# Another machine model behind the scheduler that orders a four-layer decoder trunk

## The chip, the cores and the metric

The kernel runs on one core of a Trainium2 chip. TensorE does the matmuls (its records are called PE, its weight loads PEld), VectorE (DVE) and ScalarE (ACT) do elementwise work and move results out of PSUM, GpSimd (POOL) does a few small steps, and SyncE (SP) issues the DMAs. Each engine works through its own list of instructions in the order in which they were placed there, and waits at semaphores for what the others make. The metric is device microseconds of one execution, from the median of several runs; lower is better.

## The reference

The input is one sequence of 256 positions of width 1024, in float32. Four layers follow each other. Each has a token mixer and then a SwiGLU feed-forward part (FFN); behind each of the two stands a layer norm of `ALPHA * x + h`. The mixers of layers 0 to 3 are HGRN2, mLSTM, S5 and HGRN2 again.

```python
for i in range(DEPTH):
    kind = i % N_MIXERS
    if kind == 0:
        h = _hgrn2_mixer(x, ...)
    elif kind == 1:
        h = _mlstm_mixer(x, ...)
    else:
        h = _s5_mixer(x, ...)
    x = _layernorm(ALPHA * x + h, ln_g[i, 0], ln_b[i, 0])
    x = _layernorm(ALPHA * x + _swiglu(x, ffn_w_gate_up[i], ffn_w_down[i]), ln_g[i, 1], ln_b[i, 1])
return x

def _swiglu(x, w_gate_up, w_down):
    gate, up = jnp.split(x @ w_gate_up, 2, axis=-1)
    return (jax.nn.silu(gate) * up) @ w_down
```

The HGRN2 mixer is a gated linear recurrence with 8 heads of 128: queries, gates, values and output gates are projections of x, scores between positions are weighted by products of gates, and the normalised heads are projected out. The mLSTM mixer is a matrix memory with exponential gates and a short causal convolution; S5 is a complex diagonal state space in 64 groups. The FFN has 2816 hidden units and is the largest part of the arithmetic.

## The kernel before

**Precision and loads.** Every large product is made of three: both operands are split into a high part that TensorE takes as it is and a low rest, and `mm3` (L152 to L157) adds high by high, low by high and high by low. The weights come from DRAM one megabyte at a time: `stage_next` (L97) issues the DMA on SP's queue (L106) into one of three staging buffers, and `halve` (L126) splits it, the high part on ScalarE (L127), the rest on VectorE (L128). `wstage` keeps this one entry ahead of its use (`AHEAD = 1`), in the order of a plan of all weights (`plan`, L1219). The split parts go to a pool of eight buffers each.

```python
def halve(self, x, hi, lo):
    self.nc.scalar.copy(hi, x)
    self.nc.vector.tensor_tensor(lo, x, hi.bitcast(F32), ALU.subtract)
```

**Stages.** The 256 positions are two halves of 128 rows. `as_part` (L159) multiplies x, transposed, with 512 columns of weights for one or both halves; `ws_block` and `ws_wide` (L172, L180) hold the weights in the array instead and stream both halves of x; `ws_wide` does so for the middle blocks of the FFN (L185 with 512 columns, L188 with 256). PSUM has three kinds of banks: two called "g" (projections), two called "t" (transposes) and four called "a" (scores and sums that last).

The FFN (`ffn`, L266) goes over 11 blocks of 256 hidden units: gate and up products, silu and product, and the down product added into four banks. Its layer norm (`norm`, L214) runs under `high_priority()`; for each half it takes statistics on VectorE, a reciprocal root on GpSimd (L197, L198), scales (L235, L236), transposes on TensorE (L240) and splits the result on ScalarE and VectorE (L259, L260).

HGRN (`hgrn`, L446) projects, then runs the scores of two pairs of heads side by side in seven levels. One level (`hgrn_scores`, L582) is a strided copy on ScalarE (L616), small matmuls (L620, L629), a masked copy on VectorE (L623) and the products of gates (L592). Between the levels the calls hand in pieces of the remaining projections. S5 (`s5`, L1063) goes over eight blocks: input matmuls (L1115), rotations and a scan on VectorE (L1158 to L1169) and output matmuls (L1127). The matrices of S5 are computed ahead, in pieces that run among the FFN blocks of layers 0 and 1 (`s5_prepare`, L842), and pass through DRAM.

**What sets the order.** The kernel names the engine of every instruction, but not its place. While the `with tile.TileContext(...)` block closes, the framework's scheduler places the instructions: it runs the traced program on a model of the chip and gives each engine, out of what is ready on that model, the one with the best priority, which is the order of the calls except inside `high_priority()`. It also places the tiles in the buffers of their pools and draws the waits. Two edges are drawn by hand: each load of an activation table comes behind the users of the table before and ahead of its own users (`table` and `act`, L77 to L95). The program has no control flow; it is one list of instructions.

## Time and profile before

| what | value |
|---|---|
| median of 3 runs | 1273.06 us (1273.02 to 1274.07) |
| the profiled execution's own time | 1272.88 us |
| its span, first to last instruction | 1271.1 us |
| mean granted clock of TensorE | 0.999 |
| instructions | 20366 |
| read from DRAM | 234.99 MB |

The profiled execution is 0.18 us under the median, and 1.8 us of it lie outside the span. In the profile an engine's busy time is the union of its instructions' records. The end of a matmul's record is modelled, and the records of matmuls that follow each other overlap, so a TensorE that is busy throughout need not run at its peak. L12 means line 12 of the kernel. Tiles are named by the program without their buffer numbers: w is a staging buffer, hi and lo its split parts, xx the split and transposed x.

### The profile page before, as it was taken

Reading aid. Unit: us, or ns where it says so; the run is one execution under the profiler, and the core shown is the slowest. Engines: PE = TensorE matmul, PEld = TensorE weight load, DVE = VectorE, ACT = ScalarE, POOL = GpSimd, SP = SyncE. Lnnn points to the kernel's source line nnn. Section 1 sums busy time; section 2 is a strip of 40 time slices with the busy share of each in tenths; the row PEclk is TensorE's granted clock in tenths of the full one; section 3 lists DMA queues with packets and bytes.
Section 4 is the critical chain, followed back from the end, with each engine's and each line's share of the span. In section 5 each row is a group of like instructions: output and inputs, shape, how many; then the busy total and the mean of one; then the engine's idle time right before and its main releaser. Section 6 shows DMA issues by size and latency. Waiting matters only on the chain.

```text
span 1271.1 us, 20366 instructions
## 1 busy us (share of the span) xinstructions
PE 1252.0 (98%) x7939; PEld 1047.4 (82%) x7939; DVE 958.8 (75%) x1716; ACT 711.9 (56%) x1158; POOL 54.6 (4%) x78
## 2 busy tenths in 40 slices
PE   9999999999999999999999999999999999999997
PEld 7977788888798888888878778888879778888885
DVE  6877889876787799866599797666595887766664
ACT  6755576675467555666443355555459654555550
POOL 0000200000200110000000000000010001000001
PEclk9999999999999999999999999999999999999999
DMA  8733465765373276756477647555554432755530
GB/s 312 293 134 134 159 223 207 274 243 199 113 277 134 100 259 224 246 207 244 163 273 277 244 166 247 184 199 183 182 189 185 165 121 106 271 173 192 193 139 33
DMA packets 46463, 249.93 MB, mean 197 GB/s; under 512 B 5632, under 2 KB 10128, under 8 KB 20000
## 3 DMA queue, kind: packets, MB, share of 16 engines
q1 hardware_dynamic: 46240, 248.55, 54.4%
q8 instruction: 62, 1.02, 0.3%
q14 instruction: 33, 0.27, 0.1%
q0 software_dynamic: 128, 0.09, 0.0%
HBM read 234.99 MB, written 13.63 MB: 196 GB/s over the span
## 4 chain that ended last, share of the span: by engine, by line
PE 92%; DVE 3%; ACT 2%; issue 1%; POOL 1%; DMA 0%; POOLq 0%; DVEq 0%; ACTq 0%
PE g L185 19%; PE g L155 10%; PE g L157 10%; PE g L156 10%; PE g L188 10%; PE a L155 9%; PE a L156 9%; PE a L157 8%; PE t L240 1%; PE t L1127 1%; PE g L1115 1%; DVE lo L128 1%; PE a L620 1%; PE t L1024 1%; PE a L505 0%
## 5 line engine op out<-in xcount | busy, mean ns | idle before, releaser
L128 DVE TENSOR_TENSOR lo<-w,hi 128x1024 fp32r<-128x1024 f32 x389 | 472.7, 1222 | 115.3 <-ACT hi L127 108.3
L127 ACT CAST hi<-w 128x1024 fp32r<-128x1024 f32 x389 | 406.6, 1051 | 189.0 <-PE a L156 109.1
L185 PE MATMUL g<-xx,hi 128*128 128x512 f32 x1024 | 358.3, 395 | 0.0
L188 PE MATMUL g<-xx,lo 128*128 128x256 f32 x1024 | 267.5, 281 | 0.0
L185 PEld LDWEIGHTS g<-xx,hi 128*128 128x128 f32 x1024 | 186.9, 188 | 34.3
L188 PEld LDWEIGHTS g<-xx,lo 128*128 128x128 f32 x1024 | 192.4, 188 | 10.4
L155 PE MATMUL g<-hi,xx 128*128 128x512 f32 x416 | 169.3, 408 | 4.0 <-ACT xx L259 2.9
L156 PE MATMUL g<-hi,xx 128*128 128x512 f32 x416 | 166.6, 401 | 0.0
L157 PE MATMUL g<-lo,xx 128*128 128x512 f32 x416 | 166.4, 403 | 0.0
L156 PE MATMUL a<-hi,hl 128*128 128x512 f32 x344 | 135.8, 395 | 0.0
L155 PE MATMUL a<-hi,hh 128*128 128x512 f32 x344 | 135.5, 396 | 0.0
L157 PE MATMUL a<-lo,hh 128*128 128x512 f32 x344 | 135.4, 394 | 0.0
L319 ACT COPY sum<-g 128x256 f32<-128x256 f32 x128 | 47.6, 372 | 141.3 <-PE g L185 141.0
L320 DVE TENSOR_TENSOR sum<-g,sum 128x256 f32<-128x256 f32 x128 | 54.3, 424 | 67.2 <-ACT sum L319 66.7
L155 PEld LDWEIGHTS g<-hi,xx 128*128 128x128 f32 x416 | 78.8, 190 | 22.9 <-ACT xx L259 4.7
L157 PEld LDWEIGHTS g<-lo,xx 128*128 128x128 f32 x416 | 78.7, 189 | 17.9 <-DVE lo L128 0.7
L156 PEld LDWEIGHTS g<-hi,xx 128*128 128x128 f32 x416 | 78.9, 190 | 16.0 <-issue 0.2
L156 PEld LDWEIGHTS a<-hi,hl 128*128 128x128 f32 x344 | 64.8, 188 | 14.9 <-DVE hl L309 0.3
L157 PEld LDWEIGHTS a<-lo,hh 128*128 128x128 f32 x344 | 64.7, 188 | 14.8
L155 PEld LDWEIGHTS a<-hi,hh 128*128 128x128 f32 x344 | 64.3, 188 | 13.7 <-ACT hh L308 0.6
L156 PE MATMUL g<-xx,lo 128*128 128x256 f32 x200 | 56.6, 283 | 0.0
L157 PE MATMUL g<-xx,hi 128*128 128x256 f32 x200 | 56.5, 283 | 0.0
(303 smaller groups left out, 1779.4 us busy)
## 6 DMA issues: line engine op xcount, KB each, us to landing
w<-in_w_gu SPq DMA_DIRECT2D x88, 1024.0 KB, 4.9
w<-in_w_dn SPq DMA_DIRECT2D x44, 1024.0 KB, 4.9
w<-in_w_hg SPq DMA_DIRECT2D x30, 1024.0 KB, 5.1
w<-in_w_ml SPq DMA_DIRECT2D x12, 1024.0 KB, 4.9
gb<-in_ln SPq DMA_DIRECT2D x8, 1024.0 KB, 4.7
w<-in_w_ho SPq DMA_DIRECT2D x8, 1024.0 KB, 4.9
w<-in_w_so SPq DMA_DIRECT2D x8, 1024.0 KB, 6.2
ct<-s5ct SPq DMA_DIRECT2D x8, 768.0 KB, 7.8
```

The source lines that it names most:

```text
L127: self.nc.scalar.copy(hi, x)
L128: self.nc.vector.tensor_tensor(lo, x, hi.bitcast(F32), ALU.subtract)
L155: mm(ps, lh, rh, start=start, stop=False)
L156: mm(ps, ll, rh, start=False, stop=False)
L157: mm(ps, lh, rl, start=False, stop=stop)
L185: whole = lambda: mm(ps, hi[:, c], self.xx[:, k].rearrange("p i t -> p (i t)"), start=k == 0, stop=k == KD - 1)
L188: mm(ps[:, S:], lo[:, c], self.xh[:, k], start=False, stop=False)
L240: nc.tensor.transpose(pt[:, (k % 4) * P : (k % 4 + 1) * P], z[:, k * P : (k + 1) * P], self.ident)
L319: nc.scalar.copy(t, ps[:, S:])
L320: nc.vector.tensor_tensor(t, ps[:, 0:S], t, ALU.add)
L620: nc.tensor.matmul(pl[rows(c)].rearrange("p (h a t) -> p a h t", h=2, a=2)[:, i], kk[:, i * P + 32 * c : i * P + 32 * c + 32], view(q, i * ...
L1024: nc.tensor.transpose(ps[:, x * P : (x + 1) * P], k["bz"][:, i, 4 * e + x].rearrange("p j g c -> p (j g c)"), self.ident)
```

## The change

One argument is added where the framework's context is made. It tells the scheduler to run the program on the framework's timeline machine instead of its core machine. The calls that make up the program, their engines, their operands, their priorities and the pools stay as they are.

```diff
     out = nc.dram_tensor("out_x", [S, D], F32, kind="ExternalOutput").ap()
-    with tile.TileContext(nc) as tc:
+    with tile.TileContext(nc, schedule_with_timeline_sim=True) as tc:
         trunk(tc, aps, out)
```

## The prediction

> **What bounds the kernel now.** I read the page first, for the shares of the engines and for the chain of work that ended last.
>
> ```profile
> span 1271.1 us, 20366 instructions
> PE 1252.0 (98%) x7939; PEld 1047.4 (82%) x7939; DVE 958.8 (75%) x1716; ACT 711.9 (56%) x1158; POOL 54.6 (4%) x78
> PEclk9999999999999999999999999999999999999999
> PE 92%; DVE 3%; ACT 2%; issue 1%; POOL 1%; DMA 0%; POOLq 0%; DVEq 0%; ACTq 0%
> ```
>
> The reader is to see one bound: TensorE is busy for 1252.0 of 1271.1 us, its granted clock is full in every slice, and 92% of the last chain is matmuls. No order of the same 7939 matmuls makes them fewer, so an order can only move the time in which TensorE does not work. That time is found stage by stage in the view by stretches (length, then busy us of PE, PEld, DVE, ACT and POOL, granted clock, DMA share, GB/s).
>
> ```profile
> 0.00:53.00 53.00, 50.94 (x375) 45.98 (x375) 36.34 (x42) 41.19 (x59) 1.74 (x8) 1.00 0.85 319
> 53.00:120.00 67.00, 65.71 (x869) 52.40 (x858) 56.14 (x148) 37.98 (x77) 2.08 (x2) 1.00 0.41 147
> 335.00:389.00 54.00, 53.24 (x341) 47.34 (x341) 48.92 (x98) 33.92 (x53) 2.98 (x4) 1.00 0.57 209
> 632.00:660.00 28.00, 26.74 (x124) 20.70 (x123) 26.83 (x47) 15.05 (x21) 3.43 (x4) 1.00 0.65 253
> 660.00:748.00 88.00, 85.72 (x573) 69.80 (x572) 75.31 (x125) 33.31 (x42) 1.72 (x2) 1.00 0.60 221
> 748.00:930.00 182.00, 182.00 (x920) 153.26 (x919) 119.10 (x165) 93.39 (x145) 2.64 (x4) 1.00 0.55 196
> 930.00:985.00 55.00, 53.80 (x379) 49.20 (x378) 40.08 (x58) 43.25 (x71) 3.29 (x5) 1.00 0.58 214
> 985.00:1050.00 65.00, 63.67 (x872) 50.05 (x871) 55.44 (x146) 38.78 (x79) 2.08 (x2) 1.00 0.40 146
> 1261.70:1271.10 9.40, 1.43 (x7) 0.81 (x5) 5.78 (x9) 0.00 (x0) 1.68 (x2) 0.84 0.15 56
> sum 1271.10, PE 1252.03 PEld 1047.37 DVE 958.82 ACT 711.86 POOL 54.60; mean PE 78.25 PEld 65.46 DVE 59.93 ACT 44.49 POOL 3.41
> ```
>
> Length less busy gives the idle time. In all it is 1271.10 - 1252.03 = 19.1 us. The first stretch has 2.1 of it (the first load) and the last 8.0 (the closing layer norm, one dependent chain). That leaves 9.0 us inside, of which six stretches hold 1.29 + 0.76 + 1.26 + 2.28 + 1.20 + 1.33 = 8.1: both score stages of HGRN, the three seams from an FFN into the next mixer, and the S5 blocks. The FFN stretch 748 to 930 has none at all: four such stages are most of the kernel, and order has nothing to give there.
>
> [...]
>
> ```profile
> L128 DVE TENSOR_TENSOR lo<-w,hi 128x1024 fp32r<-128x1024 f32 x389 | 472.7, 1222 | 115.3 <-ACT hi L127 108.3
> L127 ACT CAST hi<-w 128x1024 fp32r<-128x1024 f32 x389 | 406.6, 1051 | 189.0 <-PE a L156 109.1
> L185 PE MATMUL g<-xx,hi 128*128 128x512 f32 x1024 | 358.3, 395 | 0.0
> L155 PE MATMUL g<-hi,xx 128*128 128x512 f32 x416 | 169.3, 408 | 4.0 <-ACT xx L259 2.9
> L156 PE MATMUL g<-hi,xx 128*128 128x512 f32 x416 | 166.6, 401 | 0.0
> L157 PE MATMUL g<-lo,xx 128*128 128x512 f32 x416 | 166.4, 403 | 0.0
> L156 PE MATMUL a<-hi,hl 128*128 128x512 f32 x344 | 135.8, 395 | 0.0
> ```
>
> Matmuls of one shape take 395 ns in the FFN (L185, and L156 into "a") and 408, 401 and 403 in the projections (L155 to L157 into "g"). I take the excess as hidden waits: 416 x (13 + 6 + 8) ns = 11.2 us. So order can return at most 9.0 + 11.2 = 20.2 us, 1.6%, and lose without such a limit.
>
> **The change part by part.** It removes and adds no instruction: 7939 matmuls, 389 pairs of L127 and L128 and every DMA stay, so the sum of the work moves by 0. What may move is each engine's order. The kernel's trace of calls gives a priority (earlier calls first, the layer norms before others), and while the program is built, a model of the chip decides what is ready when an engine comes free. A product is passed over only where that model has its operands late. The edit exchanges the model, hence the places where something is passed over. Where that happens now, the waits of TensorE tell (us in total, times, longest), and the timeline shows one of them:
>
> ```profile
> PE g L155 <- ACT xx L259: 2.9, 5, 0.7
> PE a L620 <- DVE near L623: 2.3, 2, 1.2
> PE t L1127 <- DVE s5hs L1168: 1.3, 1, 1.3
> PE g L155 <- ACT hi L127: 0.9, 1, 0.9
> ```
>
> ```profile
> 94.73 0.40 PE L156 MATMUL g<-hi,xx 128*128 128x512 f32 x1
> 96.30 0.33 PE L620 MATMUL a<-q,kk 128*32 128x32 f32 x16 [1.18 <-DVE near L623]
> 96.56 0.50 PE L157 MATMUL g<-lo,xx 128*128 128x512 f32 x1
> ```
>
> At 94.73 the score step L620 was set too early: TensorE stands 1.18 us, and the next product of the same projection (96.56) stands behind it.
>
> The costs, in turn. **(a) TensorE's own order** in the FFNs: 0, since no stretch there has idle time; the cover is the weight pair split one plan entry ahead. **(b) Order on VectorE and ScalarE** at the six exposed places. Both engines carry the dependent chain and also the splits of weights, which nothing interrupts once begun: 1.222 us on VectorE (L128), 1.051 on ScalarE (L127). The chain at one seam shows what that is like (start, us):
>
> ```profile
> 639.79 1.14 DVE lo L128
> 640.92 0.33 DVE xx L260
> 641.59 1.13 DVE lo L128
> 643.39 1.13 DVE lo L128
> ```
>
> Three splits already lie in this chain. A different readiness puts one more before the chain or takes one out. Behind a split that is put in front wait L260 and the transposes' users on VectorE, and for them the first matmuls of the next projection. Bounds for one place: from -1.35 (the 8.1 us over six places, all regained) to +2.27 (a split on each of both engines). No row of before shows the other order, so this is a choice: one more split of 1.222 us on VectorE at three of the six places, nothing net at the other three: +3.7 us. I lean to loss because five of the six places hold no more than 1.33 us of idle time to give back, while a split on each engine costs 2.27. **(c) Hidden waits**: between -11.2 (all gone) and +11.2 (doubled); near nothing, I take a tenth more, +1.1. **(d) The load queue.**
>
> ```profile
> SPq L106 <- DVE lo L128: 554.1, 102, 21.7
> ```
>
> SP issues each load when a staging buffer is free, so its order is that of the splits. A load moved behind a late split lands late by that split, 1.2 us, and is hidden by the other two staging buffers: 0, and up to 1.2 per place without that cover, inside the bound of (b). POOL is busy 54.6 us and stands only in the layer-norm and head-norm chains, which keep their own order: 0. **(e) Head and tail**: 0; both are one chain of dependent steps with nothing to reorder.
>
> Sum: 3.7 + 1.1 = 4.8 us on the profiled execution's own 1272.88 us, 1277.7. The median of the runs is 1273.06, 0.18 above it, so the forecast is **1277.9 us**, with a range of its own from 1275.6 to 1286.8 (six places at 2.27, 13.6 us).
>
> **The rivals.** *Better aimed order, faster.* The mechanism is the row at 94.73: if the new model has L623 (and L1168 in S5) as late as the chip has it, TensorE takes projection products first and L620 and L1127 afterwards. It decides at these three waits, and it pays as long as there is another product with its weights split; here there is one. It returns 2.3 + 1.3 whole and, for the seams, where TensorE has little else, half of 2.9 + 0.9: 5.5 us, 1267.6. With all 7.4 us of these waits and a quarter of the hidden 11.2, it is 10.2 us, 1262.9. For it speaks that the waits are there and that something stands behind them; against it, that the chains behind are VectorE's, which the new order may as well lengthen.
>
> *No change.* The order may come out the same where it matters, or a gain here pay for a loss there: 1273.1. The FFN rows with no idle time speak for it; against it, that nearly all idle time is in places ruled by order.
>
> *Committed too early, much slower.* A model in which an engine's sequencer takes products before the array is free would choose among what is ready then, and a score step that becomes ready a moment later goes behind products already chosen. The projections are used up early and the later score steps stand bare. One level is these four rows in turn:
>
> ```profile
> L592 DVE TENSOR_TENSOR q<-q,f 128x256 f32<-128x256 f32 (+2 forms) x56 | 24.6, 438 | 0.0
> L592 DVE TENSOR_TENSOR k<-k,f 128x256 f32<-128x256 f32 (+1 forms) x48 | 19.0, 399 | 0.2
> L616 ACT COPY kk<-k 128x256 f32<-128x256 f32 x40 | 15.7, 413 | 11.5 <-DVE k L592 7.9 <-PE a L620 3.5
> L623 DVE COPY_PREDICATED near<-msk,a 128x64 f32<-128x64 int32 x40 | 10.2, 256 | 4.4 <-PE a L620 3.7
> ```
>
> That is 0.438 + 0.399 + 0.413 + 0.256 = 1.51 us a level; there are 7 levels in each of two runs in each of two layers, 28 steps, 42 us. Half of them bare gives 21 us, 1294.1. It decides where fewer than 1.51 / 0.23 = 6.5 matmuls are left between two levels (0.23 us is one matmul's step in the rows below). Nothing in the trace of before speaks for or against how the new model chooses.
>
> *The clock falls.* TensorE starts slowly in this trace: the chain has one matmul each at
>
> ```profile
> 8.16 0.43 PE g L155
> 8.84 0.23 PE g L155
> ```
>
> 0.43 us and then 0.23. Were bare steps long enough to bring that back, each return would cost some 8 matmuls x 0.20 = 1.6 us; ten of them on top of the last rival give 1310. The largest wait inside is 1.3 us and no stretch inside has a clock under 1.00, while the last one, nearly idle, has 0.84. [...]
>
> **How the numbers follow.** Forecast 0.36, better aimed 0.31, no change 0.21, committed early 0.10, clock 0.02. Faster is 0.31, same 0.21, slower 0.36 + 0.10 + 0.02 = 0.48; the bound between them, 0.2% or 2.5 us, is about what a measurement of this kernel can tell from no change. The predicted time is the forecast's, 1277.9. The range from 1263 to 1292 holds the forecast, no change and most of the faster case; it leaves out some 0.05 of that, and 0.10 of the two last.
>
> **What would show it.** Right: PE's busy time within 1 us of 1252.0 plus the hidden waits, idle time grown in the six stretches, with L128 ahead of L260 or the score chain, and FFN stretches with none. The faster rival: the rows L620 <- L623 and L1127 <- L1168 are gone or short. No change: the same waits at the same places. Early commitment: long runs of projection matmuls, then score steps with idle time before each. Wrong altogether would be idle time in an FFN, or waits for a DMA, since both were costed at nothing.

## The result, and the profile after

The changed kernel takes **1376.38 us** (median of 4 runs, 1374.92 to 1377.7) where the kernel before takes 1273.04 beside it: a ratio of 1.0809, with a 95% interval from 1.0791 to 1.0828. The forecast was 1277.9 with a range from 1263 to 1292. The sign is right, and the size is missed twentyfold: 103 us are lost where 4.8 were expected.

The page of the changed kernel first: span, busy time, granted clock, and the chain that ended last.

```profile
span 1375.4 us, 20399 instructions
PE 1284.7 (93%) x7939; PEld 1075.1 (78%) x7939; DVE 963.8 (70%) x1716; ACT 705.0 (51%) x1155; POOL 50.1 (4%) x78
PEclk9998899999999999999998999999999989999998
PE 84%; DVE 11%; ACT 2%; issue 2%; POOL 1%; DMA 0%; POOLq 0%; DVEq 0%; ACTq 0%
```

The work is the same: 7939 matmuls, 1716 instructions on VectorE; ScalarE's 1155 instructions instead of 1158 are three loads of an activation table fewer (15 instead of 18), so the prediction's "removes and adds no instruction" was not quite right. TensorE's idle time grows from 19.1 us to 1375.4 - 1284.7 = 90.7, its busy time by 32.7, together the 104.3 us by which the span grew. VectorE holds 11% of the chain instead of 3%, and the granted clock is no longer full in every slice. The view by stretches (columns as in the prediction; stretches with little or no idle time are left out) shows where.

```profile
104.00:132.00 28.00, 19.14 (x329) 15.38 (x331) 20.72 (x65) 8.51 (x24) 2.00 (x2) 0.76 0.13 47
132.00:159.00 27.00, 23.06 (x141) 18.96 (x130) 16.45 (x28) 10.74 (x17) 4.69 (x5) 0.94 0.28 93
159.00:186.00 27.00, 21.83 (x94) 17.11 (x93) 24.81 (x88) 14.45 (x31) 3.54 (x6) 0.87 0.33 118
186.00:358.00 172.00, 172.00 (x944) 144.23 (x943) 130.02 (x229) 105.09 (x174) 1.81 (x1) 1.00 0.65 225
358.00:388.00 30.00, 22.31 (x93) 16.56 (x92) 19.94 (x51) 7.57 (x14) 6.21 (x10) 0.89 0.30 107
487.00:510.00 23.00, 17.64 (x77) 13.62 (x76) 22.02 (x69) 5.58 (x14) 3.62 (x6) 0.85 0.38 137
684.00:713.00 29.00, 22.97 (x96) 17.31 (x95) 22.74 (x43) 8.49 (x14) 2.30 (x4) 0.88 0.91 360
713.00:806.00 93.00, 87.09 (x558) 72.11 (x557) 72.42 (x113) 31.86 (x38) 0.00 (x0) 0.94 0.47 168
806.00:828.00 22.00, 15.42 (x65) 11.77 (x64) 15.63 (x34) 6.80 (x12) 3.36 (x4) 0.84 0.47 185
1000.00:1028.00 28.00, 22.01 (x100) 16.86 (x99) 21.89 (x42) 9.15 (x16) 3.69 (x7) 0.88 0.40 149
1110.00:1169.00 59.00, 44.23 (x498) 35.31 (x498) 41.06 (x102) 22.71 (x51) 5.96 (x6) 0.88 0.23 87
1169.00:1195.00 26.00, 21.05 (x90) 16.51 (x89) 16.33 (x32) 7.32 (x15) 0.74 (x2) 0.87 0.32 122
1357.00:1375.40 18.40, 8.22 (x36) 6.15 (x34) 11.69 (x20) 0.37 (x1) 3.36 (x4) 0.81 0.15 57
```

The row from 186 to 358 is an FFN: still no idle time, as the prediction had it, and so are the other three. Three rows are what stands at the end of the HGRN scores and behind them (104, 132 and 1110): 8.9 + 3.9 + 14.8 = 27.6 us idle, of which 8.8 are the head norms (L413 in the waits below). Seven are the seams, layer norms between a mixer and an FFN or the other way round (159, 358, 487, 684, 806, 1000, 1169): 5.2 + 7.7 + 5.4 + 6.0 + 6.6 + 6.0 + 5.0 = 41.9. The S5 blocks (713) have 5.9 (2.3 before) and the tail 10.2 (8.0 before). Every row here with idle time also has a lower clock. The waits of TensorE (total us, times, longest) name what it waits for:

```profile
PE t L240 <- DVE xx L260: 18.3, 6, 4.6
PE t L240 <- DVE x L236: 16.2, 7, 6.4
PE t L413 <- DVE on L519: 8.8, 4, 3.9
PE a L620 <- DVE q L592: 8.2, 6, 1.8
PE a L620 <- DVE near L623: 4.2, 3, 2.0
```

Most of it is VectorE: the norms' transposes (L240), the head norms (L413) and the score steps (L620). These five rows hold 55.7 of the 90.7 us.

And the 32.7 us of busy time? They are the clock. The trace records the granted clock itself; in the changed kernel it is at 0.50 in fifteen stretches inside the kernel and in the tail, before in the tail alone (its record begins 9.9 us into the changed kernel and 8.5 us into the one before, behind the start with steps of 0.43 us that both have). The longest of these stretches and the sum of all sixteen (TensorE alone: length, busy, granted clock, DMA share, GB/s):

```profile
119.09:129.33 10.24, 8.57 (x83) 0.50 0.01 2
sum 99.20, PE 70.19; mean PE 4.39
```

TensorE is busy for 70.2 us at a granted clock of 0.50, where a step of 512 columns takes 0.43 us instead of the 0.23 at 1.00. At 1.00 the same matmuls would take about 70.2 x (1 - 0.23 / 0.43) = 33 us less, an estimate that is as large as the whole growth. So some 72 of the 104 us are waits, and some 33 are matmuls at 0.50 behind these waits.

Why do the score steps wait? Each of the next rows is a stretch between one score step and the next, with the matmuls that read xx alone (the projections): first the changed kernel, then the one before.

```profile
65.12:70.19 5.07, 5.07 (x21) 3.88 (x21) 0.00 (x0) 0.00 (x0) 1.00 0.31 92
```

```profile
90.91:92.96 2.05, 2.05 (x8) 1.42 (x8) 0.00 (x0) 0.00 (x0) 1.00 0.00 0
```

Counted over the scores of the first layer, the changed kernel has its projections in eight runs between the score matmuls, four of them of exactly 21 products, and none behind the eighth; before, there are over twenty runs of 1 to 12, with 2 to 4 products still between late steps. A step's chain needs far less cover than 21 (6.5 products by the prediction's estimate), so the products are used up early, and the last steps stand bare. TensorE's timeline there (start, duration, idle time before it and what ended it):

```profile
116.83 0.80 PE L620 MATMUL a<-q,kk 128*32 128x32 f32 x32 [0.81 <-DVE near L623]
119.63 0.91 PE L620 MATMUL a<-q,kk 128*32 128x32 f32 x32 [2.00 <-DVE near L623]
```

At a seam it is the norm that stands bare, and behind S5 it also lasts longer. VectorE's timeline there, the changed kernel first, then the kernel before (some rows left out):

```profile
802.40 0.69 DVE L221 SCALAR_TENSOR_TENSOR x<-x,ho 128x512 f32<-128x512 f32 x1
803.01 1.22 DVE L128 TENSOR_TENSOR lo<-w,hi 128x1024 fp32r<-128x1024 f32 x1
...
805.35 1.21 DVE L128 TENSOR_TENSOR lo<-w,hi 128x1024 fp32r<-128x1024 f32 x1
...
807.08 1.21 DVE L128 TENSOR_TENSOR lo<-w,hi 128x1024 fp32r<-128x1024 f32 x1
...
808.32 2.31 DVE L128 TENSOR_TENSOR lo<-w,hi 128x1024 fp32r<-128x1024 f32 x2
811.14 1.67 DVE L235 SCALAR_TENSOR_TENSOR x<-x,mv,gb 128x256 f32<-128x256 f32 x4
813.33 1.67 DVE L236 SCALAR_TENSOR_TENSOR x<-x,rs,gb 128x256 f32<-128x256 f32 x4
```

```profile
737.39 1.42 DVE L221 SCALAR_TENSOR_TENSOR x<-x,ho 128x512 f32<-128x512 f32 x2
...
740.03 1.17 DVE L128 TENSOR_TENSOR lo<-w,hi 128x1024 fp32r<-128x1024 f32 x1
741.12 0.88 DVE L235 SCALAR_TENSOR_TENSOR x<-x,mv,gb 128x256 f32<-128x256 f32 x2
742.04 0.88 DVE L236 SCALAR_TENSOR_TENSOR x<-x,rs,gb 128x256 f32<-128x256 f32 x2
```

Before, one split lies in this norm. Now there are five, four of them more (4 x 1.2 = 4.9 us). And TensorE has no products left beside it: it stands 6.4 us (the longest wait of the row L240 <- x L236). Before, it had them; the stretch of that norm and what follows it:

```profile
736.00:758.00 22.00, 22.00 (x102) 17.54 (x101) 20.95 (x38) 12.73 (x17) 2.63 (x4) 1.00 0.50 185
```

Here both have their part: the chain is longer, and its cover is gone.

The other seams are of two kinds. Take the chain of the first half from its statistics (L222) to its first L260, the step that TensorE's transposes wait for. At the four seams behind a mixer this chain now holds four splits instead of one, and lasts 10.8 to 13.3 us instead of 5.7 to 7.1. At the three seams behind an FFN it holds two splits instead of three and lasts 8.8 to 10.3 us instead of 8.1 to 8.3; there it is mostly the cover that is missing. An example of the first kind is the seam behind the first HGRN layer, where TensorE stands 4.0 us, until 166.53, for L260; VectorE is at splits from 161.06, 162.59 and 164.94. The last of them and the step behind it:

```profile
164.94 1.21 DVE L128 TENSOR_TENSOR lo<-w,hi 128x1024 fp32r<-128x1024 f32 x1
166.06 0.42 DVE L260 TENSOR_TENSOR xx<-t,xx 128x256 fp32r<-128x256 f32 x1
```

### The profile page after: what moved, and what is told of

Read it like the earlier page. It is cut to its first block, busy times and chain, and to the rows that moved or that the text cites. A ratio compares the mean times of both kernels' runs of the same rounds, so it can differ in the third digit from the quotient of the medians.

```text
span 1375.4 us, 20399 instructions
## 1 busy us (share of the span) xinstructions
PE 1284.7 (93%) x7939; PEld 1075.1 (78%) x7939; DVE 963.8 (70%) x1716; ACT 705.0 (51%) x1155; POOL 50.1 (4%) x78
## 4 chain that ended last, share of the span: by engine, by line
PE 84%; DVE 11%; ACT 2%; issue 2%; POOL 1%; DMA 0%; POOLq 0%; DVEq 0%; ACTq 0%
PE g L185 17%; PE g L156 10%; PE g L155 10%; PE g L157 9%; PE g L188 9%; PE a L155 7%; PE a L156 7%; PE a L157 7%; DVE lo L128 3%; DVE x L221 1%; PE t L1127 1%; DVE st L222 1%; PE g L1115 1%; PE t L240 1%; DVE x L236 1%
## 5 line engine op out<-in xcount | busy, mean ns | idle before, releaser
L185 PE MATMUL g<-xx,hi 128*128 128x512 f32 x1024 | 362.4, 395 | 0.0
L188 PE MATMUL g<-xx,lo 128*128 128x256 f32 x1024 | 267.3, 281 | 0.0
L155 PE MATMUL g<-hi,xx 128*128 128x512 f32 x416 | 169.5, 416 | 4.7 <-ACT xx L259 3.3
L156 PE MATMUL g<-hi,xx 128*128 128x512 f32 x416 | 171.1, 413 | 0.0
L155 PE MATMUL a<-hi,hh 128*128 128x512 f32 x344 | 131.6, 397 | 1.4 <-ACT hh L308 1.4
L155 PEld LDWEIGHTS g<-hi,xx 128*128 128x128 f32 x416 | 80.4, 195 | 23.9 <-ACT xx L259 4.5
L157 PEld LDWEIGHTS g<-lo,xx 128*128 128x128 f32 x416 | 81.7, 196 | 18.3 <-issue 0.2
L156 PEld LDWEIGHTS g<-hi,xx 128*128 128x128 f32 x416 | 82.4, 198 | 16.8
L259 ACT CAST xx<-t 128x256 fp32r<-128x256 f32 x56 | 20.5, 372 | 87.1 <-PE t L240 82.7
L240 PE MATMUL t<-ident,x 128*128 128x128 f32 x112 | 24.9, 314 | 34.6 <-DVE xx L260 18.3
```

The costliest lines, as they stand in the source:

```text
L155: mm(ps, lh, rh, start=start, stop=False)
L156: mm(ps, ll, rh, start=False, stop=False)
L157: mm(ps, lh, rl, start=False, stop=stop)
L185: whole = lambda: mm(ps, hi[:, c], self.xx[:, k].rearrange("p i t -> p (i t)"), start=k == 0, stop=k == KD - 1)
L188: mm(ps[:, S:], lo[:, c], self.xh[:, k], start=False, stop=False)
L240: nc.tensor.transpose(pt[:, (k % 4) * P : (k % 4 + 1) * P], z[:, k * P : (k + 1) * P], self.ident)
```

## The experiments

Two theories of the order and one of the loads were to be told apart. *Choosing ahead*: the timeline machine has a queue for each engine, whose size the runs below set; if what has gone into it is not reordered any more, an instruction with a better priority that becomes ready later goes behind it. *Durations*: the machine prices the instructions wrongly, so that it has a chain ready at the wrong time, whatever the queue. *Loads*: SP's order is the harm. All ratios are against runs of the kernel before on the same chip.

**Smaller queues.** The sizes are set ahead of the context; a, v and p are the sizes for ScalarE, VectorE with GpSimd, and TensorE.

```diff
+    from concourse.engine_type import EngineType as E
+    from concourse.hw_specs import TRN2Spec
+
+    TRN2Spec.ENG_ISSUE_QUEUE_DEPTH = {E.SP: 12, E.Activation: a, E.DVE: v, E.PE: p, E.Pool: v}
```

All sizes 1:

> [...] Theory A, choice too early: the instructions are chosen while others still wait in the queue, so what becomes ready a moment later comes behind them. Then this run gives back most of the 103 us: 1270 to 1290 us, with 3 to 12 projection matmuls between two score levels instead of 21 and no layer-norm seam with more than 2 us of idle TensorE. Theory B, prices: the timeline machine has other durations and semaphore delays, and the order follows from these. Then the time stays above 1350 us. Theory C, clock: idle stretches halve TensorE's clock, and the loss feeds itself; it can be at most the some 15 us of matmuls at 0.43 us in the changed kernel, whatever this run shows.

Measured: 1494.22 us, 1.1722 (1.1701 to 1.1743): far worse, not better. Its bound of 15 us for the clock in the changed kernel counts matmuls of 512 columns alone; over all shapes it is some 33 us, as shown above. TensorE alone at 1:

> The timeline machine with a queue of 1 for TensorE alone; VectorE, ScalarE and GpSimd keep 12. Theory A in the form that TensorE's early choice is the cause (21 matmuls ahead of each score level): back to 1270 to 1290 us. Theory A in the form that VectorE's and ScalarE's early choice is the cause in the layer norms (five weight splits inside the chain of one norm): only the idle time at L620 and L629, some 25 to 35 us, comes back, and the L240 waits stay: 1335 to 1350 us. Theory B: above 1350.

Measured: 1497.95 us, 1.1759 (1.1735 to 1.1782). The projection runs were indeed short (2 to 12 products, counted between the score steps in TensorE's order), but other things went wrong. A stretch inside an FFN of this kernel, then one of its waits:

```profile
200.00:380.00 180.00, 161.36 (x845) 134.76 (x844) 122.56 (x219) 95.75 (x157) 1.80 (x1) 0.93 0.53 184
```

```profile
PE g L155 <- DVE hd L296: 21.9, 3, 11.2
```

The FFN itself now stands 18.6 us, and on the product with the gate (L296): something in the order of VectorE or ScalarE, or of TensorE against them, is wrong that was not before. So these two runs don't decide on choosing ahead; they change a second thing.

The elementwise engines alone at 1, TensorE at 35:

> The timeline machine with a queue of 1 for VectorE, ScalarE and GpSimd; TensorE keeps 35. Theory A by TensorE: above 1350 us. Theory A by the elementwise engines: the waits of L240 (34.6 us in the changed kernel) and of L413 (8.8) go and the score levels stay bare, 1300 to 1325 us. Theory B: above 1350.

Measured: 1339.86 us, 1.0518 (1.0497 to 1.0539): some 37 of the 103 us come back, less than theory A by the elementwise engines had. VectorE alone at 1:

> The timeline machine with a queue of 1 for VectorE alone. If the weight splits put into the norm chains on VectorE (L128 between L221, L222 and L235) are the larger part, this is within 10 us of the run with all three elementwise engines at 1; if ScalarE's early choice matters as much, it lies halfway between that run and the changed kernel's 1376.

Measured: 1344.59 us, 1.0555 (1.0534 to 1.0576), so most of that, 32 us, is VectorE. In the kernel with all three at 1 the waits say what it is:

```profile
PE t L240 <- DVE x L236: 6.5, 8, 3.7
PE t L240 <- DVE xx L260: 3.4, 3, 1.3
```

The norms' waits fall from 16.2 + 18.3 to 9.9 us, and the head norms' (L413) are gone. Between the first half's statistics and its first L260 no split is left at five of the seven seams; one is at the first behind an FFN, and behind S5 three of four stay. That fits splits that were queued before the norm's steps were ready. The score steps keep their waits.

**Taking over an order.** Here the program is built twice. The first build uses one machine, and the order in which it put each engine's instructions is noted; the second uses the other machine and is held to that order on the engines listed, by edges that only order two instructions of one engine and add no wait.

```diff
+    engines = (mybir.EngineType.PE, mybir.EngineType.DVE, mybir.EngineType.Activation,)
+    orders = None
+    for timeline in (False, True):
...
+        with tile.TileContext(nc, schedule_with_timeline_sim=timeline, name="trunk") as tc:
+            trunk(tc, aps, out)
+            traced = [i for i in nc.cur_bb.bb.instructions if i.engine in engines]
+            if orders is not None:
+                for order in orders:
+                    for x, y in zip(order, order[1:]):
+                        dep = mybir.DependencyInfo(mybir.DependencyClass.NoSync, mybir.DependencyReason.DATA)
+                        tc.add_manual_dep(traced[y], traced[x].name, dep, reason="taken order")
```

The timeline machine, with TensorE, VectorE and ScalarE held to the core machine's order:

> The timeline machine schedules, but edges that order without a wait hold TensorE, VectorE and ScalarE to the order that the core machine gives them; loads, GpSimd, buffers and waits are left to the timeline machine. If the order on these three engines is the whole cause: 1270 to 1278 us. If the order of the loads or the placing of tiles carries part of it: above 1290 us.

Measured: 1289.83 us, 1.0119 (1.0099 to 1.0139). What is left are two waits of a size that neither kernel has at these places:

```profile
PE g L1115 <- DMA bm<-s5b: 7.7, 1, 7.7
PE g L155 <- ACT f L89: 3.7, 1, 3.7
```

The matrices of S5 come late, and so do first projections; the run with the loads held, below, shows that this is the order of the loads. TensorE alone held (the list of engines has PE only):

> TensorE alone is held to the core machine's order; the rest is chosen by the timeline machine. If TensorE's order is the cause (21 matmuls ahead of each score level): 1273 to 1290 us. If the weight splits in VectorE's chains are: 1330 us or more. By the run with the queue of the elementwise engines at 1, which gave back 36 of 103 us, I expect both to count: 1300 to 1340 us.

Measured: 1337.07 us, 1.0489 (1.0468 to 1.051). VectorE and ScalarE alone held:

> VectorE and ScalarE are held to the core machine's order; TensorE is chosen by the timeline machine. If TensorE's order is the cause: above 1340 us. If the elementwise engines' is: 1273 to 1290 us. If both count and each needs the other: the two losses, of this run and of the one with TensorE held, do not add up to 103 us.

Measured: 1389.01 us, 1.0897 (1.0875 to 1.0919): good orders on the elementwise engines alone give nothing back. I take it that TensorE's order then no longer fits them. Its largest wait is inside the FFN:

```profile
PE t L303 <- DVE hd L296: 24.2, 4, 6.8
```

The other way round: the core machine, with TensorE held to the timeline machine's order (`(True, False)` in the loop, PE only):

> The core machine schedules, with TensorE held to the timeline machine's order. If TensorE's order is the cause by itself, the loss of 103 us comes back: 1350 us or more. If VectorE's and ScalarE's early choices are, it stays below 1300 us.

Measured: 1373.6 us, 1.0776 (1.0754 to 1.0797). TensorE's order alone brings 99 us of loss, though every other engine is ordered by the core machine around it (anew: VectorE and ScalarE too have another order than in the kernel before). The harms of the two orders do not add up: 99 by TensorE's alone, 63 where TensorE's is the old one and the rest is new, 103 together. And the timeline machine with SP held as well as the three:

> As the run with TensorE, VectorE and ScalarE held to the core machine's order, with SyncE's loads held to it too. In that run TensorE waits 7.7 us once for S5's input matrices (L1115 for bm) and 3.7 us once at the first projections (L155 for ScalarE's f), 11.4 of the 15 us that are left. If the order of the loads is the rest of the cause: 1272 to 1277 us, and both waits are gone. If the placing of tiles or the waits drawn are: it stays at 1285 or more.

Measured in ten runs: 1273.57 us, 0.9997 (0.9987 to 1.0006). With the order of four engines taken over, the loss is gone. So **the order is the whole of it**; nothing else of what the machine decides (the buffers of the pools, the waits drawn, GpSimd's order) costs anything that can be measured here. The clock is no second cause beside it: with the old order the granted clock is back at 0.997 (0.999 before, 0.964 in the changed kernel). The first waits of this kernel are those of the kernel before, with the DMA's gone:

```profile
PE g L155 <- ACT xx L259: 2.9, 5, 0.7
PE a L620 <- DVE near L623: 2.4, 2, 1.2
```

The order of the loads is the one thing held in this run and not in the run with three engines held: 1289.83 - 1273.57 = 16 us.

**Queues of a middle size.** TensorE 8, the others 12; then TensorE 8 with the elementwise engines at 2; then 4 with 2:

> The timeline machine with a queue of 8 for TensorE alone, 12 for the others. With 1 the run came out at 1498 us although its score levels had few projection matmuls between them; I take it that a queue of 1 also keeps the model's TensorE from overlapping its steps, so that it is slow there and the elementwise engines are ordered for a slow TensorE. Theory A (choice too early): with 8 the model's TensorE overlaps again, some 7 to 16 matmuls stand between two levels, and the time falls below the changed kernel's: 1300 to 1345 us. Theory B (the model's prices): 1350 or more.

> The timeline machine with a queue of 8 for TensorE and of 2 for VectorE, ScalarE and GpSimd. Theory A: both early choices are short, so nearly all comes back but the 15 us that the order of the loads costs: 1285 to 1305 us. Theory B: not below 1340, the run with the elementwise queues at 1.

> The same with 4 for TensorE. Theory A with nothing else: a little below the run with 8. If a short queue slows the model's TensorE, as I take it for 1: above the run with 8, with waits of TensorE for VectorE inside the FFN stages (L303 for hd, L185 for sum), as at 1.

Measured: 1331.67 us, 1.045 (1.043 to 1.0471); 1309.5 us, 1.0276 (1.0256 to 1.0297); 1304.4 us, 1.0236 (1.0211 to 1.0262). With TensorE's queue the projection runs shrink (14, 9, 12, 7, 13 and 11 with 8 and 2, instead of the runs of 21), and with them the time: 45 us from the changed kernel to the run with 8, 22 more from 12 to 2 on the others, 5 more from 8 to 4, the last a small step for two runs each. The run with 8 and 2 lies a little outside what theory A had. So smaller queues give back 72 of the 103 us. That is the share of choosing ahead if a queue of this size does nothing else; that a queue of 1 does something else, the next runs show. What is left in the last is mostly small waits at the seams, the first of them:

```profile
PE t L240 <- DVE x L236: 8.1, 9, 2.3
```

**What the queue of 1 did.** TensorE's order held to the core machine's, as in t_pe, the elementwise queues at 2, and TensorE's at 1 or at 8; TensorE's order is the same in both, so only the other engines' can differ:

> TensorE is held to the core machine's order, and the timeline machine has a queue of 1 for TensorE and 2 for VectorE, ScalarE and GpSimd. With TensorE's order fixed, its queue can act only through how fast the model's TensorE is, that is through the order of the elementwise engines. If a queue of 1 makes the model's TensorE slow (my reading of the 1498 us): clearly above the sister run with 8, by 50 us or more, with waits for VectorE inside the FFN stages. If the 1498 us came from TensorE's own order: both runs within 10 us of each other.

> The sister run: TensorE held to the core machine's order, queues of 8 for TensorE and 2 for the elementwise engines. The run with TensorE held and the framework's queues took 1337 us. Theory A (choice too early on the elementwise engines too): 1290 to 1310 us, near the 1289.8 us of all three engines held. Theory B, that the rest comes from the model's prices: still above 1325 us.

Measured: 1447.07 us, 1.1354 (1.1333 to 1.1374), and 1328.99 us, 1.0427 (1.0408 to 1.0446). The 118 us between them are thus not TensorE's order. A queue of 1 thus also changes how the elementwise engines are ordered, and for the worse; I take it that TensorE runs late in the machine then, which no run shows by itself. So the two runs with 1 above tell nothing against choosing ahead. The run with 8 came out where its expectation had theory B, above 1325: it is only 8 us under the 1337.07 of the run with the queues as they come, so with TensorE's order forced, the early choice on the elementwise engines is a small part of what remains. A forced order also shifts the times that the machine sees, so this doesn't carry over to the free case, where the same queues gave 22 us.

**The loads again.** Queues 8 and 2, with SP held to the core machine's order:

> Queues of 8 for TensorE and 2 for the elementwise engines, which took 1309.5 us, with SyncE's loads held to the core machine's order. If the loads cost the same 15 us here as with the engines held: 1292 to 1298 us. If the loads' cost is hidden behind other waits here: 1305 us or more.

Measured: 1314.75 us, 1.0315 (1.0297 to 1.0334): not as expected, 5 us slower than without. The 16 us of loads shown above are not a part that can be taken off elsewhere, which suggests that load order and the order of the splits belong together.

**A better order by hand.** The core machine, held to its own order but for five projection products that are moved ahead of the score step that waits most, in both HGRN layers:

```diff
+            pe = orders[0]
+            for at in (748, 5820):
+                pe[at : at + 21] = pe[at + 8 : at + 11] + pe[at + 19 : at + 21] + pe[at : at + 8] + pe[at + 11 : at + 19]
```

> The core machine, with TensorE, VectorE, ScalarE and SyncE held to its own order, except that in both HGRN layers five projection matmuls are taken ahead of the score step at which TensorE stands 1.18 us in the kernel before (94.73 to 96.30). This is the first place of the faster rival. If it holds: 2 x 1.1 us less than before, about 1270.9 us, and the two waits of L620 for L623 gone. If the chain behind is lengthened as much: 1273 us.

Measured in eleven runs: 1272.98 us, 0.9993 (0.9984 to 1.0002): no difference that can be measured, and not the 2.2 us hoped for. The wait of 2.3 us became two:

```profile
PE a L620 <- ACT kk L616: 1.1, 2, 0.5
PE a L620 <- DVE near L623: 1.0, 2, 0.5
```

The waits at the score step still add up to 2.1 us, at other places of its chain. No order tried here beats the kernel before.

## Why the prediction was wrong

**What bounds the kernel, and (a), TensorE in the FFNs: right.** The four FFN stretches have no idle time after the change either. The work is the same, and an order can lose without the limit that it has on the side of gain.

**(b), order on VectorE and ScalarE: the step that failed.** It took one more split of 1.222 us at three of six places, 3.7 us in all, with a bound of 2.27 for each, 13.6 in all; TensorE's idle time grew by 71.6. At each of the seven seams it is now 5.0 us or more. Three things were wrong in it. The *bound* was taken from one split on each engine: behind a mixer there are three more in the chain, behind S5 even four if it is counted from the addition (L221), and nothing in the trace of before limits how many can be ready ahead of a chain. The *cost* was taken to be splits alone: behind an FFN the chain has one split fewer than before, and TensorE still stands 6.0 to 7.7 us, because it has no products left beside it. And the *places* were those that wait now; the four norms behind the mixers didn't wait, so they were left out, though they have the same chain. They hold 22 of the seams' 42 us.

**(c), hidden waits: the second step that failed.** TensorE's busy time was to stay within 1 us of 1252.0 plus the hidden waits, which were taken as 1.1 us more; it grew by 32.7, and that is the granted clock of 0.50. No run shows the 11.2 us of hidden waits that the term started from. In the trace of before, that excess comes from 110 of the 1248 projection matmuls: eight stand in the start with its steps of 0.43 us (1.9 us), and nearly all others directly behind small matmuls of a score step or a transpose, where a record lasts 0.47 to 0.51 us instead of 0.40, as the row at 96.56 in the prediction does behind L620. The clock was among the rivals, but it was judged by the longest wait of the kernel before, 1.3 us; the new order made waits of up to 6.4.

**(d), the load queue: open in size.** Costed at nothing. With the other orders held it is 16 us (1289.83 against 1273.57), with queues of 8 and 2 holding it gave nothing back; in the changed kernel itself there is one wait for a DMA, 1.7 us, of L1115 for S5's matrices. How much of the 103 us the order of the loads is there was not measured.

**(e), head and tail: nearly right.** The head is unchanged and the tail loses 2.2 us.

**The rivals.** What happened is *committed too early*, with a chance of 0.10: long runs of projection matmuls, then score steps with idle time before each, just as the list of signs had it. Its 21 us for the scores were near the 27.6 idle there, or the some 19 without the head norms. It missed that the same early choice strikes each norm (41.9 us) and brings *the clock falls* with it, the last rival, which had 0.02 and put ten returns at 16 us: there were fifteen, and some 33 us. The sentence that nothing in the trace speaks for or against how the new model chooses was true; but then the forecast's bounds and its chance of 0.36 had no ground either. A bound on the safe side would have been the bare chains, what all score steps, norms and head norms cost when TensorE has nothing beside them, and on top of that the matmuls at 0.50 behind them. That a loss was forecast and not a gain came from a lean of the chances (0.48 for slower), so the right sign is in part luck.

**What stays open.** With queues of 4 and 2 the timeline machine's order is still 30 us behind the core machine's. Whether that is its durations, what remains of the queues, or something else was not settled; the run with TensorE's order held and queues of 8 and 2, at 1328.99 us, speaks for the durations as much as for the queues. The durations of the two machines were not exchanged in any run.

## What to carry to other kernels

A priority only works where the choice is made late: with the changed kernel's queues, products meant as cover came in runs of 21 here (7 to 14 with queues of 8 and 2), and the chains that they should have covered stood bare at the end. When an order is changed, bound the loss by the length of all dependent chains that are covered now, not by the waits that show now, and add what the clock takes behind such waits, a third of the loss here by the estimate above. To learn which engine's order matters, take over the noted order engine by engine, in both directions, since the parts need not add up.

## What was not expected of the hardware

The granted clock falls in the middle of this kernel, which the prediction held for nearly excluded. Every stretch at 0.50 inside the changed kernel lasts 3.4, 6.8 or 10.2 us, and those at 1.00 between them last 2 to 58 times 3.41 us. So the trace can be cut into pieces of 3.41 us that begin and end where the clock changes. The pieces around the end of the scores (TensorE alone: length, busy, granted clock, DMA share, GB/s):

```profile
112.26:115.68 3.42, 2.06 (x60) 1.00 0.00 0
115.68:119.09 3.41, 1.00 (x48) 1.00 0.00 0
119.09:122.50 3.41, 2.11 (x38) 0.50 0.02 5
122.50:125.92 3.42, 3.06 (x39) 0.50 0.00 0
125.92:129.33 3.41, 3.41 (x9) 0.50 0.00 0
129.33:132.74 3.41, 3.41 (x45) 1.00 0.00 0
```

No single wait here is over 2.00 us (the timeline above). Yet the clock is at 0.50 behind a piece in which TensorE was busy for 1.00 of 3.41 us, and it stays there for 10.2 us, until the end of the first piece in which TensorE was busy throughout. The whole trace looks like that: all fifteen falls inside the kernel come behind a piece with TensorE busy for at most 45%, and all fifteen returns behind one with 97% or more (one such piece, from 736.90, brought no return).

At the seam behind S5 it is a single long wait that stands ahead of a fall: TensorE waits 6.4 us there, until 813.96, and the clock is at 0.50 from 811.99 on, behind a piece without a matmul:

```profile
808.58:811.99 3.41, 0.00 (x0) 1.00 0.75 250
811.99:815.40 3.41, 1.31 (x5) 0.50 0.89 365
```

In the rows above it is little work over several short waits. What the clock goes by, beyond these counts, no run here shows.
